# Gate and up projections: two 256-column matmuls in place of a 512-column one, for three column tiles of four

## The chip, the core and the metric

The kernel runs on one core of one Trainium2 chip. The metric is the device time of one execution in microseconds; the time before is the median of three runs. Profiles are of one execution each, with every instruction's start and length on each engine: TensorE (PE, and PEld for its weight loads), VectorE (DVE), ScalarE (ACT), GpSimd (POOL), and SyncE (SP), which issues the DMAs.

## The reference

One decoder layer over 256 tokens (`SEQ`) of width 2048 (`D_MODEL`): four token mixers with a common input and output projection, then a gated ConvFFN of width 5632. All in float32. What matters here is the second half:

```python
h = rmsnorm(x, norm_ffn[l]) * (1.0 + sc2) + sh2
x = x + g2 * conv_ffn(h, ffn_w_gate[l], ffn_w_up[l], ffn_conv_w[l], ffn_conv_b[l], ffn_w_down[l])
...
def conv_ffn(h, w_gate, w_up, conv_w, conv_b, w_down):
    gate = causal_dwconv(h @ w_gate, conv_w) + conv_b
    return (jax.nn.silu(gate) * (h @ w_up)) @ w_down
```

`h @ w_gate` and `h @ w_up` are the two projections that the change touches: 256 x 2048 by 2048 x 5632 each.

## The kernel before, in words

Float32 products are made of parts. Each operand is split into a high part of type fp32r and the remainder (`split`: a ScalarE cast to `wh`, line 115, and a VectorE subtraction to `wl`, line 100), and three products are summed: high by high, high by low, low by high. The rounded parts of the layer's input lie side by side in `H2` (the tile `bigA` in the trace): for each of the 16 K tiles of 128 rows, columns 0 to 255 hold the high part of the 256 tokens and columns 256 to 511 the low part.

The stages follow each other: modulation and the combined input projection (tiles `acc` and `ext`), the mixers, the output projection (`wot`), gate and up, and the down projection (both with PSUM tiles `fpt`). Gate and up loop over 11 blocks of 512 columns. For each block `proj` runs twice, first with the gate's weights, then with the up's. A projection takes four PSUM tiles `a[0]` to `a[3]` of 128 x 512, one for each column tile of 128 columns, and goes through the 16 K tiles. Weights come in loads of two K tiles (512 KB, `load_split`), with three buffers each for `wh` and `wl` and five for the raw `wr`. In each K tile four matmuls have the 128 x 128 block of `wh` as weights and all 512 columns of `H2` moving: columns 0 to 255 of the PSUM tile gather high by high, columns 256 to 511 high by low. Four more have `wl` as weights and the 256 high columns moving, and add into columns 0 to 255. Every matmul has a weight load of its own.

When a projection is through, the two halves of each PSUM tile are summed: ScalarE copies the second half to `lo` (line 1040) and VectorE adds it to the first. Then comes, for each of the four column tiles, the convolution and gating: `cv` (two buffers) is made from the gate's PSUM tile by a ScalarE activation and two VectorE operations, passes Silu, is multiplied with the up's PSUM tile, and is split to `AH` and `AL` for the down projection. There are eight PSUM buffers for `fpt`, four for gate and four for up, so a block's gate tiles take the place of those of the block before.

The order of the instructions on each engine is set by the tile framework's planner, which runs the program on a simulated timeline and lets an engine take whatever is ready there by its estimates; so the order in a K tile or between blocks need not be that of the source. The combined input projection (`gdn` and `pair` in the source) has the same three products, written as three matmuls of 256 columns with one sum: `wh` by high, `wh` by low, `wl` by high. The last two column chunks of the down projection are of 256 columns too, with `AH` and `AL` as the weights and `wh` and `wl` moving.

All matmuls are recorded at line 97, in the helper `mm`, and VectorE's `tensor_tensor` at line 100, so groups are told apart by their tiles.

Of the kernel before, what the change touches and what calls it, by code (L numbers as in the profile page):

```python
# [8 lines left out]
F32 = mybir.dt.float32  # L9
# [3 lines left out]
ALU = mybir.AluOpType  # L13
# [3 lines left out]
P = 128  # L17
D = 2048
KT = D // P
T = 256  # L20
# [53 lines left out]
def trunk_kernel(ctx: ExitStack, tc: tile.TileContext, x, c, w_mod, b_mod, norm_mix, norm_ffn, w_in,  # L74
# [4 lines left out]
    V, S_, G, PE = nc.vector, nc.scalar, nc.gpsimd, nc.tensor  # L79
# [16 lines left out]
    def mm(o, l, r, start=True, stop=True):  # L96
        PE.matmul(o, lhsT=l, rhs=r, start=start, stop=stop, skip_group_check=True)  # L97

    def tt(o, a, b, op):
        V.tensor_tensor(out=o, in0=a, in1=b, op=op)  # L100
# [57 lines left out]
    def load_split(view, k0, nk, c0, n):  # L158
        wr = load(view, k0, nk, c0, n)
        wh = wp.tile([P, 1024], F32R, name="wh", tag="wh", bufs=3).rearrange("p (k n) -> p k n", n=n)  # L160
        wl = wp.tile([P, 1024], F32R, name="wl", tag="wl", bufs=3).rearrange("p (k n) -> p k n", n=n)
        split(wh[:, 0:nk], wl[:, 0:nk], wr[:, 0:nk])
        return wh, wl
# [64 lines left out]
    with ExitStack() as ph:  # L228
# [59 lines left out]
        with ExitStack() as st:  # L288
# [19 lines left out]
            b = ext()  # L308
            PE.transpose(b[:, 0:KT], crow, ident[:KT, :KT])
            act(cond, b[:, 0:KT], AF.Silu)  # L310
            b = ext()
# [11 lines left out]
            for k in range(0, KT, 2):  # L323
                b = ext().rearrange("p (k t) -> p k t", t=T)
# [653 lines left out]
        with tc.tile_pool(name="op", bufs=2, reuse_waits="tile") as op:  # L978
            for n, (c0, w) in enumerate(chunks):
                ns, gs = slice(c0, c0 + w), slice(c0 % 1024, c0 % 1024 + w)  # L980
                a = a0
                if n > 0:
                    a = [wop.tile([P, 512], F32, name="wot", tag="wot")[:, 0:w] for _ in range(NT)]
# [8 lines left out]
    with ExitStack() as ph:  # L992
        fpp = ph.enter_context(tc.tile_pool(name="fpp", bufs=8, space=PSUM, reuse_waits="tile"))
        fpt = lambda: fpp.tile([P, 512], F32, name="fpt", tag="fpt")
        H2 = bigA()
        with tc.tile_pool(name="hp", bufs=2, reuse_waits="tile") as hp:
# [9 lines left out]
            for k in range(0, KT, 2):  # L1006
                b = fpt().rearrange("p (k t) -> p k t", t=T)
# [17 lines left out]

        def proj(gp, view, c0):

            a = [fpt() for _ in range(4)]
            for g in range(KT // 2):
                wh, wl = load_split(view, 2 * g, 2, c0, 512)  # L1030
                for kk in range(2):
                    k = 2 * g + kk
                    fs = lambda f: slice(f * P, f * P + P)
                    for f in range(4):
                        mm(a[f], wh[:, kk, fs(f)], H2[:, k], start=k == 0, stop=False)
                    for f in range(4):
                        mm(a[f][:, 0:T], wl[:, kk, fs(f)], H2[:, k, 0:T], start=False, stop=k == KT - 1)
            for b in a:
                lo = gp.tile([P, T], F32, name="lo", tag="lo")
                S_.copy(lo, b[:, T:])  # L1040
                tt(b[:, 0:T], b[:, 0:T], lo, ALU.add)
            return [b[:, 0:T] for b in a]

        with tc.tile_pool(name="gp", bufs=2, reuse_waits="tile") as gp:
            for n in range(NF // 4):
                gt = proj(gp, wg_v, 512 * n)
                ut = proj(gp, wu_v, 512 * n)
                for i in range(4):
                    f = 4 * n + i
                    w3 = lambda j: V3[:, j * NF + f:j * NF + f + 1]  # L1050
                    cv = gp.tile([P, T], F32, name="cv2", tag="cv2")
                    act(cv, gt[i], AF.Identity, scale=w3(2), bias=CB[:, f:f + 1])
                    for sh in (1, 2):
                        stt(cv[:, sh:], gt[i][:, 0:T - sh], w3(2 - sh), cv[:, sh:], ALU.mult, ALU.add)
                    act(cv, cv, AF.Silu)
                    tt(cv, ut[i], cv, ALU.mult)
                    split(AH[:, f], AL[:, f], cv)
# [4 lines left out]
        with tc.tile_pool(name="op2", bufs=1, reuse_waits="tile") as op:  # L1062
            chunks = ((0, 512), (512, 512), (1024, 512), (1536, 256), (1792, 256))
            fs = op.tile([P, NT, len(chunks)], F32, name="fs")
            f1 = op.tile([P, 4], F32, name="f1")
            for n, (c0, w) in enumerate(chunks):
# [3 lines left out]
                a = [fpt()[:, 0:w] for _ in range(NT)]  # L1070
                nk = 1024 // w
                for g in range(NF // nk):
                    wh, wl = load_split(wd_v, nk * g, nk, c0, w)
                    for kk in range(nk):
                        k = nk * g + kk
# [55 lines left out]
```

## Time and profile before

| | us |
|---|---|
| median of three runs | 1303.85 |
| lowest and highest run | 1300.9, 1304.77 |
| the profiled execution | 1303.01 |
| its span in the profile | 1301.2 |
| gate and up in it, from 549.26 to 1041.95 | 492.69 |
| down projection in it, from 1041.95 to 1288 | 246 |

The span runs from the first to the last recorded instruction; about 1.8 us of the execution lie around it. In a group's row stand the number of instructions, the time for which at least one of them ran, the mean duration of one, and the idle time of the engine ahead of them with what ended it. Matmuls overlap each other, so their spacing is read from the starts in the timeline, whose rows give start, length and how many like instructions in a row are merged. A row of the windows view has the window, its length, then busy time and count for PE, PEld, DVE, ACT and POOL, the granted TensorE clock, the share of the DMA engines and GB/s. A row of the waits view says who waited for whom, the microseconds in total, how often, and the longest.

### The profile page before, as it was taken

The numbers are of one execution on the slowest core, as the hardware profiler recorded it, in microseconds if no ns is written. First come the engines' busy times: TensorE is split into PE (matmuls) and PEld (weight loads), VectorE is DVE, ScalarE is ACT, GpSimd is POOL, SyncE is SP. The second block draws the span as 40 slices with busy tenths as digits, with TensorE's granted clock in tenths as the row PEclk, the third lists the DMA queues.
The fourth block names the chain that finished last, engine by engine and source line by source line (L and its number), as shares of the span: only waits on it lengthen the run. The fifth ranks groups of instructions, "written<-read, shape, count | busy, mean of one in ns | idle before, by whom it ended". The sixth has DMA issues, their size and how long they took to land.

```text
span 1301.2 us, 20372 instructions
## 1 busy us (share of the span) xinstructions
PE 1248.5 (96%) x7927; PEld 1091.0 (84%) x7927; DVE 891.0 (68%) x1201; ACT 636.7 (49%) x1000; POOL 22.7 (2%) x31
## 2 busy tenths in 40 slices
PE   2799999999999999999999999999999999999996
PEld 1799999898876788888888888888888888888896
DVE  7689797989763397676656656665656597964543
ACT  3455344774354454564545555554555454443432
POOL 0200000010000100000000000000000000000000
PEclk9799999999999999999999999999999999999998
DMA  9999998796566988556576666666665699875652
GB/s 321 277 367 378 337 341 290 259 339 212 164 236 240 318 317 276 156 165 192 163 214 190 186 187 193 190 172 206 187 187 163 219 374 359 323 243 194 192 181 81
DMA packets 174231, 311.94 MB, mean 240 GB/s; under 512 B 16172, under 2 KB 65331, under 8 KB 173495
## 3 DMA queue, kind: packets, MB, share of 16 engines
q1 hardware_dynamic: 174135, 310.65, 72.9%
q8 instruction: 62, 1.02, 0.3%
q14 instruction: 34, 0.28, 0.1%
HBM read 308.51 MB, written 2.10 MB: 239 GB/s over the span
## 4 chain that ended last, share of the span: by engine, by line
PE 92%; DMA 4%; SPq 1%; DVE 1%; ACT 1%; issue 1%; POOLq 0%; ACTq 0%; DVEq 0%
PE fpt L97 57%; PE ext L97 16%; PE wot L97 5%; PE gdt L97 4%; PE acc L97 4%; PE bgt L97 3%; DMA wm<-in_w_mod_dram 3%; PE oxt L97 2%; DMA wr<-in_w_in_dram 1%; DVE ga L103 1%; DMA ct<-in_cst_dram 0%; ACT xT L1011 0%; DVE wl L100 0%; SPq L399 0%; SPq L155 0%
## 5 line engine op out<-in xcount | busy, mean ns | idle before, releaser
L100 DVE TENSOR_TENSOR wl<-wr,wh 128x1024 fp32r<-128x1024 f32 x384 | 469.2, 1223 | 293.6 <-ACT wh L115 292.6
L115 ACT CAST wh<-wr 128x1024 fp32r<-128x1024 f32 x384 | 403.4, 1051 | 494.9 <-PE fpt L97 310.8
L97 PE MATMUL fpt<-bigA,wh 128*128 128x512 f32 x1408 | 399.6, 395 | 2.1 <-DVE bigA L103 2.1
L97 PEld LDWEIGHTS fpt<-bigA,wh 128*128 128x128 f32 x1408 | 239.3, 189 | 32.8 <-issue 2.2
L97 PEld LDWEIGHTS fpt<-bigA,wl 128*128 128x128 f32 x1408 | 222.4, 188 | 34.4 <-DVE wl L100 3.6
L97 PE MATMUL fpt<-bigA,wl 128*128 128x256 f32 x1408 | 240.4, 279 | 0.0
L103 DVE SCALAR_TENSOR_TENSOR ga<-wm,cond,ga 128x1024 f32<-128x1024 f32 x139 | 177.8, 1279 | 9.5 <-DMA wm<-in_w_mod_dram 8.6
L97 PE MATMUL fpt<-wl,AH 128*128 128x512 f32 (+1 forms) x440 | 152.9, 348 | 0.0
L97 PE MATMUL fpt<-wh,AL 128*128 128x512 f32 (+1 forms) x440 | 152.5, 347 | 0.0
L97 PE MATMUL fpt<-wh,AH 128*128 128x512 f32 (+1 forms) x440 | 142.5, 348 | 0.0
L97 PE MATMUL ext<-bigA,wh 128*128 128x256 f32 x768 | 137.0, 280 | 0.0
L97 PEld LDWEIGHTS ext<-bigA,wh 128*128 128x128 f32 x768 | 117.3, 188 | 3.1 <-DVE dS L100 0.8
L97 PE MATMUL ext<-bigA,wl 128*128 128x256 f32 x384 | 107.2, 280 | 1.7 <-DVE wl L100 1.7
L97 PEld LDWEIGHTS fpt<-wh,AH 128*128 128x128 f32 x440 | 83.3, 189 | 10.7 <-issue 0.2
L97 PEld LDWEIGHTS fpt<-wh,AL 128*128 128x128 f32 x440 | 83.3, 189 | 10.5 <-issue 0.2
L97 PEld LDWEIGHTS fpt<-wl,AH 128*128 128x128 f32 x440 | 83.3, 189 | 10.5 <-issue 0.2
L97 PE MATMUL acc<-bigA,wh 128*128 128x256 f32 x384 | 70.3, 289 | 4.7 <-ACT bigA L115 2.9
L97 PEld LDWEIGHTS ext<-bigA,wl 128*128 128x128 f32 x384 | 72.1, 188 | 3.0 <-DVE wl L100 2.1
L97 PE MATMUL ext<-wh,bigA 128*128 128x256 f32 (+1 forms) x320 | 68.0, 304 | 0.0
L97 PEld LDWEIGHTS acc<-bigA,wh 128*128 128x128 f32 x384 | 60.7, 198 | 5.1 <-ACT bigA L115 3.0
L97 PE MATMUL wot<-wh,bigA 128*128 128x512 f32 (+1 forms) x256 | 63.2, 337 | 0.0
L97 PEld LDWEIGHTS ext<-wh,bigA 128*128 128x128 f32 x320 | 51.7, 188 | 5.5 <-ACT wh L115 1.7
(340 smaller groups left out, 1191.9 us busy)
## 6 DMA issues: line engine op xcount, KB each, us to landing
wm<-in_w_mod_dram SPq DMA_DIRECT2D x192, 512.0 KB, 5.8
wr<-in_w_in_dram SPq DMA_DIRECT2D x88, 512.0 KB, 9.7
wr<-in_ffn_w_gate_dram SPq DMA_DIRECT2D x88, 512.0 KB, 3.9
wr<-in_ffn_w_up_dram SPq DMA_DIRECT2D x88, 512.0 KB, 4.4
wr<-in_ffn_w_down_dram SPq DMA_DIRECT2D x88, 512.0 KB, 4.5
wr<-in_w_out_dram SPq DMA_DIRECT2D x32, 512.0 KB, 4.2
xt<-in_x_dram SPq DMA_DIRECT2D x2, 1024.0 KB, 7.2
bigC<-in_x_dram SPq DMA_DIRECT2D x2, 1024.0 KB, 8.6
```

What stands on the lines that cost most here:

```text
L97: PE.matmul(o, lhsT=l, rhs=r, start=start, stop=stop, skip_group_check=True)
L100: V.tensor_tensor(out=o, in0=a, in1=b, op=op)
L103: V.scalar_tensor_tensor(out=o, in0=a, scalar=s, in1=b, op0=op0, op1=op1)
L115: S_.copy(hi, src)
```

## The change

In each K tile only column tile 0 keeps the 512-column matmul. For column tiles 1 to 3 the same weights are used in two matmuls of 256 columns, `wh` by the high half and `wh` by the low half of `H2`, both into columns 0 to 255 of the PSUM tile, which the low weights' matmul adds to as before. The second half of these PSUM tiles is no longer used, so only `a[0]` is copied to `lo` and summed.

```diff
                     for f in range(4):
-                        mm(a[f], wh[:, kk, fs(f)], H2[:, k], start=k == 0, stop=False)
+                        if f == 0:
+                            mm(a[f], wh[:, kk, fs(f)], H2[:, k], start=k == 0, stop=False)
+                        else:
+                            mm(a[f][:, 0:T], wh[:, kk, fs(f)], H2[:, k, 0:T], start=k == 0, stop=False)
+                            mm(a[f][:, 0:T], wh[:, kk, fs(f)], H2[:, k, T:], start=False, stop=False)
                     for f in range(4):
                         mm(a[f][:, 0:T], wl[:, kk, fs(f)], H2[:, k, 0:T], start=False, stop=k == KT - 1)
-            for b in a:
-                lo = gp.tile([P, T], F32, name="lo", tag="lo")
-                S_.copy(lo, b[:, T:])
-                tt(b[:, 0:T], b[:, 0:T], lo, ALU.add)
+            lo = gp.tile([P, T], F32, name="lo", tag="lo")
+            S_.copy(lo, a[0][:, T:])
+            tt(a[0][:, 0:T], a[0][:, 0:T], lo, ALU.add)
             return [b[:, 0:T] for b in a]
```

## The prediction

> **What bounds the kernel now.** I read the page's busy shares first, then the chain that ended last, then the windows of the stage that the diff touches.
>
> ```profile
> span 1301.2 us, 20372 instructions
> PE 1248.5 (96%) x7927; PEld 1091.0 (84%) x7927; DVE 891.0 (68%) x1201; ACT 636.7 (49%) x1000; POOL 22.7 (2%) x31
> ```
> ```profile
> 549.25 738.94 PE fpt L97 x4141
> ```
> ```profile
> 549.26:1041.95 492.69, 492.69 (x2817) 427.66 (x2818) 311.92 (x452) 261.58 (x399) 0.00 (x0) 1.00 0.62 186
> 1224.80:1288.00 63.20, 63.20 (x527) 63.16 (x526) 30.86 (x33) 23.03 (x28) 0.00 (x0) 1.00 0.44 135
> ```
>
> From 549.25 us to 1288.2 us the chain is one piece of TensorE work. The window row cuts out gate and up: 492.69 us, TensorE busy all of it at granted clock 1.00, VectorE 311.92 us and ScalarE 261.58 us. A busy TensorE is not proof that it is at its peak, so the starts of its matmuls have to be read. The stage's groups and waits:
>
> ```profile
> L97 PE MATMUL fpt<-bigA,wh 128*128 128x512 f32 x1408 | 399.6, 395 | 2.1 <-DVE bigA L103 2.1
> L97 PE MATMUL fpt<-bigA,wl 128*128 128x256 f32 x1408 | 240.4, 279 | 0.0
> L100 DVE TENSOR_TENSOR fpt<-fpt,lo 128x256 f32<-128x256 f32 x84 | 32.7, 423 | 0.0
> L1040 ACT COPY lo<-fpt 128x256 f32<-128x256 f32 x84 | 28.6, 372 | 11.4 <-DVE fpt L100 11.4
> ```
> ```profile
> ACT wh L115 <- PE fpt L97: 188.1, 138, 1.8
> PEld fpt L97 <- DVE wl L100: 3.6, 10, 0.4
> ```
>
> ScalarE's casts wait 188.1 us for TensorE to free a weight buffer, whereas TensorE's weight loads wait 3.6 us, ten times in all, for the other two. So the stage costs what the spacing of the matmuls costs, and little else. The means of 395 and 279 ns are durations of overlapping instructions and not the spacing; that comes from the timeline of TensorE (start, length, group):
>
> ```profile
> 681.83 1.09 PE L97 MATMUL fpt<-bigA,wh 128*128 128x512 f32 x4
> 682.76 0.62 PE L97 MATMUL fpt<-bigA,wl 128*128 128x256 f32 x4
> 683.22 1.09 PE L97 MATMUL fpt<-bigA,wh 128*128 128x512 f32 x4
> 684.15 0.62 PE L97 MATMUL fpt<-bigA,wl 128*128 128x256 f32 x4
> 684.61 0.62 PE L97 MATMUL fpt<-bigA,wh 128*128 128x512 f32 x2
> 685.07 0.40 PE L97 MATMUL fpt<-bigA,wl 128*128 128x256 f32 x2
> ...
> 688.77 0.39 PE L97 MATMUL fpt<-bigA,wh 128*128 128x512 f32 x1
> 688.99 0.28 PE L97 MATMUL fpt<-bigA,wl 128*128 128x256 f32 x1
> 689.11 0.40 PE L97 MATMUL fpt<-bigA,wh 128*128 128x512 f32 x1
> ...
> 693.00 1.10 PE L97 MATMUL fpt<-bigA,wh 128*128 128x512 f32 x4
> ```
> ```profile
> 694.02 0.74 PE L97 MATMUL fpt<-bigA,wl 128*128 128x256 f32 x4
> 694.60 1.09 PE L97 MATMUL fpt<-bigA,wh 128*128 128x512 f32 x4
> ```
>
> Three forms are to be seen. A whole K tile (four 512s, four 256s) lasts 1.387 us (681.83 to 684.61, two of them): 0.93 for the 512s, 232 ns each, and 0.455 for the 256s, 114 each. At the head of a gate block six K tiles run in pieces: two column tiles first (684.61 to 688.77, six times 0.693), then the other two one by one, a 512 and its 256 in turn (689.11 to 693.00, eleven pairs, 353.5 ns each). Two pairs and 0.693 make 1.400 us for such a K tile. Last, the wait: 693.00 to 694.02 is 0.09 more than 0.93, and 694.02 to 694.60 is 0.12 more than 0.455, so each of the ten costs 0.21, and 2.1 us together.
>
> The ten waits stand in the ten blocks after the first, six K tiles in pieces each. The stage has 22 projections of 16, which is 352 K tiles: 292 whole x 1.387 = 405.0, 60 x 1.400 = 84.0, waits 2.1: 491.1 of the 492.69 us. The other 1.6 are its first matmuls.
>
> **The change, part by part.** It takes away three of a K tile's four 512s, 352 x 3 = 1056, and puts 2112 256s there, so 1056 matmuls and 1056 weight loads are added. The columns streamed stay the same. What the new 256s cost is not in this stage, where no more than four stand in a row, and has to be bounded from other stages. The same form, `wh` by the high half, the same `wh` by the low half, into one sum, runs in the combined input projection (chain rows, start, length, count):
>
> ```profile
> 114.34 16.32 PE acc L97 x144
> ...
> 167.27 16.96 PE acc L97 x144
> ```
>
> 16.32 us for 144 is 113.3 ns a matmul, 16.96 is 117.8: two gears, each held for the whole stretch. The last 256-column chunks of the down projection, with another operand as weights, take 63.20 / 527 = 119.9 (window row above). So the ends are 113.3 and 119.9. I take 113.3: the instruction of the same form shows it, and this stage's own 256s stand there too, for four that follow a 512 take 455 ns and the slow gear would make them 471.
>
> A new K tile is one 512 and ten 256s. The 512 and the first 256 behind it are the 353.5 ns of the alternating rows; nine more at 113.3 are 1020. Sum 1373, against 1387: 14 ns less in each of 292 whole tiles, -4.1 us. Of the 60 in pieces, the first two column tiles become a 512 and four 256s, 353.5 + 3 x 113.3 = 693, as before. Each of the others becomes three 256s, 340 for 353.5; 120 such are -1.6 us. **Together -5.7 us.** At 119.9 a whole tile would be 1433 and a piecewise one 353.5 + 9 x 119.9, the same 1433 against 1400: 292 x 46 + 60 x 33 = +15.4 us.
>
> Here the Trainium skill speaks against the change. Its page TensorE: Matmul & The Clock Gate, section Back-to-back issue gap, gives N / 2.4 + 2.5 ns for a warm matmul, so each split one pays the 2.5 ns twice: an estimate of 1056 x 2.5 = +2.6 us, and the sum would be +2.6 in place of -5.7. This trace does not show that fixed part in the fast gear, where two 256s are 226.7 ns and a 512 of this stage is 232.
>
> Three of the four `lo` copies and sums of each projection go: 66 x 0.372 = 24.6 us of ScalarE and 66 x 0.423 = 27.9 us of VectorE. I cost this at nothing: both engines lie beside TensorE, with 231 and 181 us to spare in the stage (window row). If that cover were absent it would be a gain, not a loss. One place lacks cover, the ten waits of 2.1 us. They come after the chain behind an up block (`lo`, sum, gating, split of `cv`, which has two buffers, so the next gate block's third and fourth PSUM tiles wait for it). With three copies fewer the pieces may shrink and the waits vanish, -2.1; or the planner, which weighs the matmuls anew, sets casts later and doubles them, +2.1. A matmul of `wl` still comes 0.92 us after the K tile begins (353.5 + 5 x 113.3 for 0.93), so I leave them at 0 and keep both ends. No DMA, no SP and no POOL instruction is added or moved. The first few K tiles' 1.6 us stay. Nothing is late next: TensorE runs on into the down projection.
>
> The profiled execution took 1303.01 us, its span 1301.2 and 1.8 around it; -5.7 makes 1297.3. It lies 0.84 under the median of the three runs, 1303.85, so for the median I say **1298.2 us**, 0.44% less.
>
> **The rivals.** (1) *The slow gear.* The 256s take 117.8 ns, as in the stretch at 167.27 us. A whole tile is 353.5 + 9 x 117.8 = 1414, +27; in pieces also 1414 against 1400, +14: 292 x 27 + 60 x 14 = +8.7, **1312.6 us**, slower. For it: both gears lasted through 144 matmuls of this very form. Against it: the 512 in each K tile breaks the run, and behind a 512 this stage shows the fast gear every time. Gain and loss balance when 5.7 / (5.7 + 8.7) = 40% of the tiles run in it; beyond that it decides.
>
> (2) *The gears mix, or every added matmul has a small price.* Half the tiles in each is +1.5, **1305.4 us**, no change. It is a mean of 2.2 ns for each of the nine 256s over the fast gear. The Trainium skill's 2.5 ns for each matmul, named above, comes out near it. For it: the two chain rows; against it: 455 ns for four.
>
> (3) *The down projection's price*, 119.9: +15.4, **1319.3 us**. For it: 527 in a row kept it with nothing waiting. Against: other operands, and no such spacing where `wh` is the weights.
>
> (4) *The loads are not hidden.* One weight load of the stage has this row:
>
> ```profile
> L97 PEld LDWEIGHTS fpt<-bigA,wh 128*128 128x128 f32 x1408 | 239.3, 189 | 32.8 <-issue 2.2
> ```
>
> 1056 more at 189 ns, bare, are +200 us, **1503 us**. Against it: in the stretch at 114.34 us 144 matmuls, each with a load of its own, start every 113.3 ns. The Trainium skill, TensorE: Matmul & The Clock Gate, section The mechanism, says that a load overlaps matmuls in flight only when its row group differs; by that stretch the trace disagrees.
>
> (5) *The change doesn't do what it says for the waits*: doubled or gone, 1300.3 or 1296.1; this widens the forecast's own range and is no case by itself.
>
> **How the numbers follow.** Forecast 0.59, slow gear 0.16, mixed 0.18, down's price 0.06, bare loads 0.01. A difference under 0.3%, 3.9 us, can't be told from none here, by runs that spread over 3.9 us. Faster: the forecast's case less a little where the waits double, 0.57. Same: the mixed case and that little, 0.20. Slower: the rest, 0.23. The forecast's own range is 1294 to 1300.8: the two ends of the waits, half a microsecond for the runs, and below it 1.6 us more, a third of what 353.5 ns lie over three 113.3s in 352 tiles (4.8 us), if a lone 512 pays less beside a run of 256s. The range reaches on to the slow gear, 1313, and leaves out 0.07 above and about 0.08 within the cases' own scatter.
>
> **What would show it.** In the profile after: `fpt<-bigA,wh` with 352 matmuls of 512 columns and 2112 of 256; 22 `lo` copies for 88; a K tile of 1.37 us in the timeline (1.41 in the slow gear, 1.43 at down's price); TensorE busy throughout gate and up, in about 487 us; PEld full, for its 427.66 us by 11 loads in place of 8 would be over the stage's length. The waits on `wl` show ten times or fewer. I am wrong if runs of ten 256s have a gear of their own, or if the planner's new order opens gaps before `wl`.

## The result, and the profile after

The changed kernel is slower: 1309.64 us (median of five, 1307.02 to 1314.29) against 1301.52 us for the kernel before (1300.17 to 1304.77), a ratio of 1.0054, 95% interval 1.0035 to 1.0073. Ratios here leave out executions more than 1.5% above their kernel's fastest; this touches only the kernel without 512s, where it is told.

The profiled execution took 1308.91 us against 1303.01. First the page (span, busy shares), then the window of gate and up, then its groups with shapes kept apart.

```profile
span 1307.1 us, 22298 instructions
PE 1254.2 (96%) x8983; PEld 1144.9 (88%) x8983; DVE 871.5 (67%) x1135; ACT 616.2 (47%) x934; POOL 22.7 (2%) x31
```
```profile
548.89:1047.79 498.90, 498.90 (x3872) 482.51 (x3873) 294.05 (x390) 242.41 (x336) 0.00 (x0) 1.00 0.62 184
```
```profile
L97 PE MATMUL fpt<-bigA,wh 128*128 128x256 f32 x2112 | 320.3, 281 | 0.0
L97 PE MATMUL fpt<-bigA,wl 128*128 128x256 f32 x1408 | 238.2, 281 | 0.0
L97 PE MATMUL fpt<-bigA,wh 128*128 128x512 f32 x352 | 140.4, 399 | 2.1 <-DVE bigA L103 2.1
L100 DVE TENSOR_TENSOR fpt<-fpt,lo 128x256 f32<-128x256 f32 x21 | 8.9, 425 | 0.0
```

Gate and up went from 492.69 to 498.90 us: +6.2, and all of the 5.9 between the two executions. TensorE is busy throughout, at granted clock 1.00 on the mean of the stage, as before. The timeline of TensorE says where the time lies; the waits of its weight loads hold one entry, 2.2 us at the stage's start, so it does not lie there:

```profile
700.11 1.11 PE L97 MATMUL fpt<-bigA,wh 128*128 128x512 f32 x7
701.05 0.63 PE L97 MATMUL fpt<-bigA,wl 128*128 128x256 f32 x4
701.52 1.11 PE L97 MATMUL fpt<-bigA,wh 128*128 128x512 f32 x7
702.47 0.64 PE L97 MATMUL fpt<-bigA,wl 128*128 128x256 f32 x4
702.94 0.52 PE L97 MATMUL fpt<-bigA,wh 128*128 128x512 f32 x2
```
```profile
PEld fpt L97 <- issue: 2.2, 1, 2.2
```

(A merged row of seven carries the form of its first: one 512 and six 256s.) A K tile lasts 1.41 us, 700.11 to 701.52 to 702.94. That is rival 1's 1414 ns and not the 1373 of the forecast. Within it the four `wl` matmuls now take 0.47 us; before the change they took 0.455. The spacings one by one, each from a start to the next, read 236 ns for the 512 and 118, 118, 117, 118 ... for the ten 256s: the slow gear, in nearly every K tile of the stage. The ten waits on `wl` are gone.

### The profile page after: what moved, and what is told of

Same layout as the page of the kernel before. It is cut to its first block, busy times and chain, and to the rows that moved or that the text cites. A ratio compares the mean times of both kernels' runs of the same rounds, so it can differ in the third digit from the quotient of the medians.

```text
span 1307.1 us, 22298 instructions
## 1 busy us (share of the span) xinstructions
PE 1254.2 (96%) x8983; PEld 1144.9 (88%) x8983; DVE 871.5 (67%) x1135; ACT 616.2 (47%) x934; POOL 22.7 (2%) x31
## 4 chain that ended last, share of the span: by engine, by line
PE 92%; DMA 4%; DVE 1%; SPq 1%; ACT 1%; issue 1%; POOLq 0%; ACTq 0%; DVEq 0%
PE fpt L97 57%; PE ext L97 15%; PE wot L97 5%; PE gdt L97 4%; PE acc L97 4%; PE bgt L97 3%; DMA wm<-in_w_mod_dram 2%; PE oxt L97 2%; DMA wr<-in_w_in_dram 1%; DVE ga L103 1%; DMA ct<-in_cst_dram 0%; DVE wl L100 0%; ACT xT L1011 0%; SPq L155 0%; ACT wh L115 0%
## 5 line engine op out<-in xcount | busy, mean ns | idle before, releaser
L97 PE MATMUL fpt<-bigA,wh 128*128 128x256 f32 (+1 forms) x2464 | 400.8, 298 | 2.1 <-DVE bigA L103 2.1
L97 PEld LDWEIGHTS fpt<-bigA,wh 128*128 128x128 f32 x2464 | 347.6, 190 | 18.6 <-issue 2.2
L97 PEld LDWEIGHTS fpt<-bigA,wl 128*128 128x128 f32 x1408 | 197.3, 189 | 0.0
L97 PEld LDWEIGHTS ext<-bigA,wh 128*128 128x128 f32 x768 | 117.7, 189 | 3.1 <-DVE E L100 0.8
```

## The experiments

Stage lengths are those of gate and up in the profile, from the first matmul to the first of the down projection. In every window below TensorE is busy for all but at most 0.25 us of it, at granted clock 1.00 on the mean, so a stage is the sum of its matmul spacings. One thing beside the change moves a stage by about 1.5 us: its head. In some executions the first 3 us or so run at about half the granted clock, with 213 ns from one 256 to the next; the kernel before, the changed one and none512 begin so, while halves, lone_once, sync, sync1 and none512_again don't. The head of the changed kernel's stage:

```profile
548.89:552.10 3.21, 3.21 (x14) 3.11 (x15) 2.70 (x7) 0.91 (x2) 0.00 (x0) 0.51 0.02 5
```

### Which property of the split matmuls is slow?

Four kernels. *Halves* splits but keeps two sums and all copies; *apart* changes the order so that neither weights nor sum repeat; *two512* splits only tiles 2 and 3; *none512* splits all four and drops all copies.

```diff
 halves:
-  mm(a[f][:, 0:T], wh[:, kk, fs(f)], H2[:, k, T:], start=False, stop=False)
+  mm(a[f][:, T:], wh[:, kk, fs(f)], H2[:, k, T:], start=False, stop=False)
 apart: tile 0's 512, then H2[:, k, 0:T] for f = 1, 2, 3, then H2[:, k, T:] for f = 1, 2, 3
 two512:
-  if f == 0:
+  if f < 2:
 none512:
-  if f == 0:
+  if False:
```

> Theories on why the 256-column matmuls of gate and up run at 117.8 ns in the changed kernel (stage 498.9 us). Same sum: two matmuls in a row that add into the same PSUM columns are slow. Same weights: the same block of wh loaded twice in a row is slow. Lone 512: a single 512-column matmul between 256s puts TensorE into the slow gear, and two or more in a row put it into the fast one. Start: the gear is set by chance where the unbroken stream of matmuls starts, and kept. Here the second of the two split matmuls goes into columns 256 to 511 as before the change, and all four copies are kept. Same sum says fast: a K tile of 1373 ns, stage 485 us. Same weights and lone 512 say slow: 1413 ns, 499 us. Start allows either.

> The changed kernel with the order of a K tile altered: the 512, then the three column tiles' high halves, then their low halves, so that neither the same weights nor the same sum come twice in a row. Same sum and same weights say fast: stage 485 us. Lone 512 says slow, 499 us. Start allows either.

> Column tiles 0 and 1 keep the 512-column matmul, only 2 and 3 are split. Lone 512: two in a row give the fast gear, as in the pieces of two before the change (226, 236, 118, 113 ns): a K tile of 226 + 236 + 118 + 7 x 113.3 = 1373 ns, stage 485 us, and some 7 us faster than the kernel before. Same sum and same weights: the five matmuls at and behind the split ones slow, 462 + 5 x 117.8 + 3 x 113.3 = 1391 ns, stage 491 us. Start: 1373 or 1413 ns, 485 or 499 us.

> All four column tiles split, no 512 left, no copies. Twelve 256s in a K tile. Lone 512: nothing forces the slow gear; the gear that the stream starts in is kept, 12 x 113.3 = 1360 ns (stage 480 us) or 12 x 117.8 = 1413 ns (499 us). Same sum and same weights: slow, 499 us. Start: either.

The four windows of the stage, in this order:

```profile
550.03:1047.46 497.43, 497.43 (x3873) 481.13 (x3873) 311.05 (x452) 260.53 (x399) 0.00 (x0) 1.00 0.62 185
```
```profile
551.58:1050.55 498.97, 498.97 (x3872) 482.62 (x3873) 294.18 (x390) 242.39 (x336) 0.00 (x0) 1.00 0.62 184
```
```profile
548.90:1033.95 485.05, 485.05 (x3520) 455.01 (x3521) 299.73 (x410) 248.66 (x357) 0.00 (x0) 1.00 0.63 189
```
```profile
548.35:1028.80 480.45, 480.45 (x4224) 480.45 (x4225) 286.51 (x370) 237.82 (x316) 0.00 (x0) 1.00 0.65 191
```

Halves 497.4 and apart 499.0 us: neither the shared sum nor the repeated weights matter, both ideas fall. (Halves is the shorter by the head, which is at full clock there; its K tiles read 236, 118, 118, 117 ... like the changed kernel's.) (Ratios to the kernel before: 1.0040, 1.0025 to 1.0055, and 1.0049, 1.0032 to 1.0067.) Two 512s in a row: 485.05 us, ratio 0.9933 (0.9918 to 0.9948). No 512 at all: 480.45 us, ratio 0.9874 (0.9854 to 0.9893), the fastest, with the most matmuls. Two512's K tile in the timeline:

```profile
700.24 1.08 PE L97 MATMUL fpt<-bigA,wh 128*128 128x512 f32 x6
701.16 0.62 PE L97 MATMUL fpt<-bigA,wl 128*128 128x256 f32 x4
701.61 1.08 PE L97 MATMUL fpt<-bigA,wh 128*128 128x512 f32 x6
```

1.37 us, 700.24 to 701.61. So splitting a 512 need not cost anything, and what seems to cost is a 512 that stands alone. One thing did not fit yet: of four executions of none512 three took 1287.0 to 1289.9 us, and one 1306.6.

### Is a gear kept, and does each 512 change it?

*Three512* splits tile 3 alone, *two_split* splits tiles 1 and 3, *lone_once* is none512 with one 512 in the whole stage, and *one_copy* is the kernel before, unsplit, with only tile 0's copy and sum; it leaves out the high by low part of the other three tiles.

```diff
 three512:
-  if f == 0:
+  if f < 3:
 two_split:
-  if f == 0:
+  if f % 2 == 0:
 lone_once: 512 only where k == 0 and f == 0, in the gate projection of block n == 1
 one_copy (on the kernel before):
-  for b in a:
+  for b in a[0:1]:
```

> Column tiles 0 to 2 keep the 512, only tile 3 is split: three 512s in a row in each K tile. Adjacent theory (a 512 alone between 256s leaves the slow gear, two or more in a row leave the fast one): 226 + 2 x 236 + 118 + 5 x 113.3 = 1383 ns, stage 488 us. Parity theory (each 512 flips the gear, an even number flips it back): K tiles alternate between 1383 and 1413 ns, mean 1398, stage 494 us.

> Two 512s in a K tile as in the run with tiles 0 and 1, but on tiles 0 and 2, with the two split matmuls of tile 1 between them. Adjacent theory: both are lone, slow gear, 1413 ns, stage 499 us. Parity theory: slow only between the two, 226 + 118 + 118 + 236 + 118 + 5 x 113.3 = 1383 ns, stage 488 us. A theory that only the number of 512s matters: as with tiles 0 and 1, 485 us.

> The kernel without 512s, but with a single 512 in the whole stage, in the first K tile of the second block's gate projection. If a lone 512 sets the slow gear and TensorE keeps a gear while its stream is unbroken, the first block stays at 1360 ns a K tile and the ten behind it go at 1413: stage 480.4 + 320 x 0.053 = 497 us. If it slows only its neighbours, or the gear has another cause, 480.5 us.

> The kernel before with all its 512s, but only column tile 0's second half is copied and added (the high by low part of the other three is left out of the result). It gives the price of the 66 copies and sums alone. Covered, as the prediction had it: spacing unchanged, stage between 490.5 us (the ten waits on wl gone) and 492.7, and the same total time within 0.2%. If copies were not covered: up to 25 us less.

Lone_once, two windows of equal length ahead of the one 512 (592.4 us) and behind it, and one far behind:

```profile
570.00:590.00 20.00, 20.00 (x179) 20.00 (x179) 9.97 (x11) 10.68 (x13) 0.00 (x0) 1.00 0.63 190
600.00:620.00 20.00, 20.00 (x172) 20.00 (x171) 10.18 (x12) 8.54 (x10) 0.00 (x0) 1.00 0.70 204
1000.00:1020.00 20.00, 20.00 (x172) 20.00 (x171) 12.22 (x18) 10.43 (x16) 0.00 (x0) 1.00 0.63 186
```

179 matmuls in 20 us become 172, and 400 us later it is still 172. One instruction of 226 ns slowed the 3838 matmuls of 256 columns behind it: every one of them takes 117 to 119 ns to the next. The stage is 495.97 us where 497 was expected, 15.5 over none512. Part of the price is hidden by the heads, slow in none512 and not here; none512_again, the same kernel as none512 with a head at full clock, has this stage:

```profile
552.29:1031.20 478.91, 478.91 (x4224) 478.91 (x4225) 286.45 (x370) 237.83 (x316) 0.00 (x0) 1.00 0.65 192
```

Against it the one 512 cost 17.1 us, and 320 x 0.053 is 17.0. Nine of the ten executions of lone_once took 1304.6 to 1309.4 us, one 1293.3 (ratio of all ten to the kernel before: 1.0020, 0.9993 to 1.0047); the one has no profile, and why it escaped stays open. That decides it: TensorE keeps a gear, and a lone 512 puts it into the slow one.

The windows of three512, two_split and one_copy:

```profile
547.46:1039.73 492.27, 492.27 (x3168) 445.52 (x3169) 304.88 (x431) 257.42 (x378) 0.00 (x0) 1.00 0.62 186
```
```profile
549.81:1043.29 493.48, 493.48 (x3520) 461.89 (x3521) 302.24 (x411) 249.36 (x357) 0.00 (x0) 1.00 0.61 186
```
```profile
549.80:1042.51 492.71, 492.70 (x2816) 427.73 (x2817) 295.21 (x390) 243.29 (x336) 0.00 (x0) 1.00 0.62 186
```

and one_copy's waits of the weight loads on VectorE:

```profile
PEld fpt L97 <- DVE wl L100: 3.7, 10, 0.4
```

Three512: 492.3 us, near parity's 494 and not the 488 of adjacency. Its K tiles alternate as parity says (spacings 225, 236, 231, then 118s; next tile 231, 229, 236, then 118 and 113s); the total time was 1.0021 (1.0004 to 1.0038). Two_split fits neither: 493.5 between 488 and 499, ratio 1.0001 (0.9983 to 1.0018). Its spacings show both patterns: K tiles of 231, 116, 114, 226 and six slow 256s at 578 us, and from 607 us ones of 226, 118, 117, 233, 122, 116 and four fast. In these each 512 does change the gear, but which stretch is fast depends on how it began. At 556 us, where the planner had put one 256 between the two 512s (236, 118, 235), all is slow, and neither 512 changes it. One_copy: nothing changes (0.9998, 0.9982 to 1.0014), stage 492.71 for 492.69. The 66 copies and sums were worth nothing, and the ten waits stay without them. Halves has all the copies and no such waits, and two_split, with half of the copies, has ten (2.1 us). So it was not fewer copies that removed the waits of the changed kernel; the planner's new order is the likely reason, which no run isolates.

Parity can't be all, or the changed kernel's K tiles would alternate. From the starts in these ten traces comes a rule. *Fast gear*: 113.3 ns for a 256; a 512 leads to the slow gear. *Slow gear*: 256s in threes, 118, 118, 117. A 512 that comes straight behind the 512, or after 0 or 2 of three, leads back to the fast gear; after 1 of three it doesn't, and the count starts again. The changed kernel has ten 256s between two 512s in 285 of 351 cases, and 4, 7, 13, 16 or 25, where the planner altered the order, in all others but two. All these are 1 of three: no way back. The two are a 6 and a 14 (0 and 2 of three), and right behind them, at 573 and 576 us, stand the only fast 256s of its stage, each time up to the next 512. The alternating rows of before have one: no way back either. Four 512s and four 256s come back, by the rule, from any start within two K tiles, and the kernel before did not stay slow.

### The rule, put to a test

Four kernels made to be told apart by the rule. *Alt01* and *alt03* have as many matmuls as the changed kernel; only the place of the 512 in odd K tiles differs. *Sync* and *lone_pair* are none512 with a few 512s.

```diff
 alt01 (alt03 with 3 for 1):
+  V.memset(a[1][:, T:], 0.0)
...
-  if f == 0:
+  if f == (0, 1)[k % 2]:
...
-  lo, copy and sum for a[0]
+  lo, copy and sum for a[0] and a[1]
 sync: in up projections, K tile 0: 512 (f=0), high half of f=1, 512 (f=2), 512 (f=3), low half of f=1
 lone_pair: K tile 0 of gate: 512 for f=0; K tile 0 of up: 512 for f=0 and f=1
```

> As many instructions as the changed kernel, one 512 in each K tile, but on column tile 0 in even and on column tile 1 in odd K tiles (column 256 to 511 of the second tile is zeroed first). The rule read from the runs so far: in the fast gear a 512 leads to the slow gear; there TensorE counts 256s in threes (118, 118, 117 ns); a 512 that comes straight behind the 512 or after 0 or 2 of three leads back to the fast gear, after 1 of three it doesn't and the count begins anew. Behind an even tile's 512 ten 256s and two of the odd tile follow, twelve, 0 of three: back to fast. Even tile 226 + 10 x 117.8 = 1404, odd tile 236 + 233 + 238 + 6 x 113.3 = 1387, mean 1395 ns, stage 493 us. If only a lone 512's presence counts: slow throughout, 1413 ns, 499 us.

> The same, with the odd K tiles' 512 on column tile 3. By the rule sixteen 256s lie between the even and the odd tile's 512, 1 of three: no way back, 1413 ns in every K tile, stage 499 us, 6 us more than with tiles 0 and 1 at the same number of instructions. If an alternating place of the 512 alone frees the gear: 493 us as there.

> No 512s but in the first K tile of each up projection, where the order is 512 (tile 0), 256 (tile 1), 512 (tile 2), 512 (tile 3), 256 (tile 1). By the rule this order ends in the fast gear from either gear and any count. Fast gear through the stage as without 512s: 480.4 us and 0.5 for the eleven places, total 1.1 to 1.3% under the kernel before, and no execution near 1306 us, as the kernel without 512s had one. If the rule is wrong, some or all of the stage is slow: up to 499 us.

> No 512s but one in the first K tile of each gate projection and two in a row in the first K tile of each up projection. By the rule the lone one makes the gate projection slow (190 matmuls of 256 columns up to the pair, 1 of three), and the pair ends in the fast gear: gate slow, up fast, stage 480.4 + 176 x 0.053 = 490 us. If a pair doesn't free the gear: 499 us. If a lone 512 slows only its neighbours: 481 us.

The stage in alt01 and alt03, and an odd and an even K tile of alt01:

```profile
549.60:1040.10 490.50, 490.27 (x3873) 476.63 (x3873) 304.13 (x432) 248.87 (x358) 0.00 (x0) 1.00 0.63 187
```
```profile
549.27:1046.90 497.63, 497.40 (x3872) 481.38 (x3873) 304.11 (x433) 248.59 (x358) 0.00 (x0) 1.00 0.62 185
```
```profile
700.12 1.09 PE L97 MATMUL fpt<-bigA,wh 128*128 128x256 f32 x7
701.04 0.62 PE L97 MATMUL fpt<-bigA,wl 128*128 128x256 f32 x4
701.50 1.10 PE L97 MATMUL fpt<-bigA,wh 128*128 128x512 f32 x7
702.43 0.64 PE L97 MATMUL fpt<-bigA,wl 128*128 128x256 f32 x4
702.90 0.63 PE L97 MATMUL fpt<-bigA,wh 128*128 128x256 f32 x3
```

490.5 and 497.6 us, 7.1 apart (6 expected) with the same 3872 matmuls and the same granted clock. The odd K tile (700.12 to 701.50) takes 1.38 us with its `wl` at 0.46; the even one 1.40 with its `wl` at 0.47. Both stages are somewhat under what was expected, 493 and 499. In alt01 the gears came as the rule has them, but the odd tile's spacings sum to 1376 ns and not to the 1387 put down. In alt03 ten pauses of some 40 ns between two 256s (159 ns for 118 at 605.7 us) each lead back to the fast gear until the next 512. Ratios 0.9974 (0.9961 to 0.9986) and 1.0034 (1.0022 to 1.0047).

Lone_pair, a window in each of two gate (600, 646) and up projections (624), and sync's order at 614.16 us, where the gear ahead was the slow one:

```profile
600.00:620.00 20.00, 20.00 (x172) 20.00 (x171) 13.78 (x22) 10.55 (x17) 0.00 (x0) 1.00 0.60 186
624.00:642.00 18.00, 18.00 (x161) 18.00 (x160) 9.40 (x11) 9.03 (x11) 0.00 (x0) 1.00 0.66 182
646.00:664.00 18.00, 18.00 (x156) 18.00 (x155) 11.78 (x20) 10.25 (x15) 0.00 (x0) 1.00 0.58 179
```
```profile
613.68 0.64 PE L97 MATMUL fpt<-bigA,wl 128*128 128x256 f32 x4
614.16 1.11 PE L97 MATMUL fpt<-bigA,wh 128*128 128x512 f32 x5
615.10 0.62 PE L97 MATMUL fpt<-bigA,wl 128*128 128x256 f32 x4
615.55 0.62 PE L97 MATMUL fpt<-bigA,wh 128*128 128x256 f32 x4
```

Lone_pair's stage: 489.76 us for 490 expected, ratio 0.9980 (0.9968 to 0.9993); slow in gate (156 in 18 us), fast in up (161). Sync's: 481.0 for 480.9, ratio 0.9916 (0.9901 to 0.9931); that the stage agrees so closely is luck, for 400 slow matmuls (1.7 us) and a head at full clock (1.5 us less) cancel. The `wl` rows frame its order: four in 0.48 us ahead (613.68 to 614.16), in 0.45 behind (615.10 to 615.55). It was slow there because in the first block the planner had put 512, 256, 512, 256, 512, which by the rule ends slow, and did, for the 400 matmuls up to the order at 614.16 us.

The rule can be followed through a whole stage, with the matmuls' order as the trace has it and each 512 moving the gear. Left out are the two 256s behind a 512 and the first few behind a gap. Behind a gap the gear is read from the trace and not forecast, and where it is the slow one, where the count is not known, again behind the next 512. So followed, the rule names the gear of all 2796 256s that are left in alt01, all 2724 in alt03, all 4113 in sync and all 4087 in lone_pair; and of all 2786 in the changed kernel, from which it was made.

### Does the order that leads back keep the gain?

```diff
 none512_again: none512 unaltered
 sync1: sync's order only in blocks n > 0
```

> The kernel without 512s once more, for how its executions spread. The first four were 1287.0, 1287.9, 1289.9 and 1306.6 us. If a gear is kept from where the stream starts or is disturbed, and nothing in this kernel leads back, executions lie at about 1288 (fast throughout), at 1306 (slow throughout), and some between; the chance is unknown. If the one at 1306.6 was something else, all lie near 1288.

> The kernel with the order 512, 256, 512, 512 in up projections, but from the second block on, since in the first one the order came out as 512, 256, 512, 256, 512, which by the rule ends slow and did. Fast throughout if the stage starts fast: 480.4 + 0.5 us; if it starts slow, slow up to the second block's up projection (48 of 352 K tiles, 2.5 us). All executions within 4 us of each other, about 1.2% under the kernel before; none near 1306 us.

None512_again: 1288.4 to 1292.3 us four times and 1309.1 once; ratio without that one 0.9897 (0.9882 to 0.9912). Sync1: 1287.9 to 1290.4, no such execution, ratio 0.9894 (0.9880 to 0.9907), stage:

```profile
548.86:1028.05 479.19, 479.19 (x4195) 477.88 (x4196) 293.97 (x397) 244.79 (x343) 0.00 (x0) 1.00 0.64 192
```

So sync1 beats both kernels by 13 us or more. The two late executions of none512 are 17 to 21 us over the others, as 352 K tiles x (1413 - 1360) ns = 18.7 us would be; but they have no profile, so that they were slow throughout is argued and not shown. That this order prevents them rests on the four executions of sync1 and the six of sync, none of them late, against two late of nine.

## Why the prediction was wrong

**The failed step** is the sum of the new K tile, "one 512 and the first 256 behind it 353.5, nine more at 113.3 are 1020". The first half held (236 + 118 = 354); the nine are at 117.7, so 1413 ns and not 1373. Over 352 K tiles these 40 ns are 14.1 us; less the 2.1 us of waits that went, they account for the 11.9 us between the -5.7 forecast and the +6.2 of the stage. The step's reason was that behind a 512 this stage shows the fast gear every time. It did so behind *four*, and behind two in a row, where the rule ends fast; the 232 ns taken for a 512 was a mean of 226, 236, 231 and 236, in which the gear had changed four times. The rows with one 512 and one 256 in turn, from which the 353.5 came, were the only ones with a lone 512, and they were the slow gear, with only one 256 in each to show it.

**Rival 1** held: slow gear nearly throughout, 1312.6 us said. The ratio of 1.0054 on the same 1303.85 is 1310.9. Its sum was +8.7; the stage gave +6.2, since the waits of 2.1 us went, the low end that the prediction had kept and not taken. Its argument against (the 512 in each K tile breaks the run) was the cause seen the wrong way round.

**The waits** went, but not for the first reason named, fewer copies: one_copy dropped the copies and kept the waits.

**The copies at nothing** held: one_copy, 0.9998.

**Rivals 3 and 4** fell. The 256s of this stage did not run at 119.9, and none512 hides twelve loads in a K tile of 1360 ns. **Rival 2's** small price for every added matmul fell too: none512 adds 1408 matmuls and its stage is 12.2 us shorter. The Trainium skill's 2.5 ns for each (TensorE: Matmul & The Clock Gate, section Back-to-back issue gap, where the figure stands for an isolated matmul) would have made it an estimated 3.5 us longer; here the measurement decides against it.

**The range** as a whole, up to 1313 us for the slow gear, held the 1309.64 us; the forecast's own, 1294 to 1300.8, did not, and the direction was forecast wrongly, at 0.57 for faster.

## What to carry to other kernels

Read matmul spacing from the starts, by what stands before each form, and not one price for each width: here the same 256-column matmul costs 113.3 or 117.8 ns by the pattern of 512s ahead of it, and one 512 cost 17 us. In a stream that is bound by TensorE, check that a mix of widths leads back to the fast gear. One width alone was as fast as any mix here, but two of its nine executions were late, and it has nothing that leads back. Here the row whose pattern was nearest to the new one (a lone 512) outweighed the row whose instruction was nearest.

## What the runs showed of the hardware that was not expected

TensorE has two spacings for gate and up's stream of fp32r matmuls with a weight load each: a 256 starts every 113.3 or every 117.7 ns. It keeps the slow one over 3838 matmuls in lone_once and the fast one through none512's stage, through changes of weights, PSUM tile and engine load, until a 512 or a gap in the stream comes (alt03's ten pauses of some 40 ns each ended the slow one). It is not the clock gate: the granted clock is 1.00 in lone_once's windows ahead and behind. The Trainium skill (TensorE: Matmul & The Clock Gate, section What's actually happening) lists two clock states, a factor of 2 apart. The heads of the stage show such a pair (213 ns at granted clock 0.51 in the changed kernel); the two gears are a factor of 1.04 apart at one granted clock. What in TensorE holds the gear stays open: the rule describes the starts, and no run here looks behind them. Open also is what sets it at the start of a stage; the chain rows of the input projection before the change had both, for the same matmuls. The down projection's 256s, with `AH` and `AL` as weights, keep a third spacing, 120 ns for 523 of the 525 from 1225 to 1288 us, which no run here explains.
